# Delta-rule layer of a hybrid decoder: 16x16 block inverses on VectorE joined by TensorE, and products in a fixed alternating order

## The chip, the cores and the metric

The kernel runs on one core of a Trainium2 chip. The metric is the device time of one execution in microseconds (us). Engines are called TensorE (PE), VectorE (DVE), ScalarE (ACT), GpSimd (POOL) and SyncE (SP); PEld is TensorE's loading of weights.

## What is computed

A trunk of four layers over 1024 steps of 1024 channels in fp32: a short convolution, an S5 layer, the delta-rule layer (RWKV-7) and a convolution again. The delta-rule layer has 16 heads of 64 channels and carries a 64x64 state per head through the steps:

```python
def _rwkv_step(state, inp):
    r_t, w_t, k_t, v_t, kk_t, a_t = inp
    sa = einsum("bhvk,bhk->bhv", state, -kk_t)
    state = (state * w_t[:, :, None, :] + sa[..., None] * (kk_t * a_t)[:, :, None, :]
             + v_t[..., None] * k_t[:, :, None, :])
    out = einsum("bhvk,bhk->bhv", state, r_t)
    return state, out
...
r, k, v, z = einsum("nbld,nde->nble", xs[:4], w_rkvz)     # xs: mixes of x with its shift
kk = heads(k * k_k) / norm;   decay = exp(-exp(w_log))
out = scan(_rwkv_step, zeros, (r, decay, k, v, kk, a))
```

## The kernel before

*Chunks.* The 1024 steps are done in two halves h of 512, the heads in 8 pairs m, so there are 16 head pairs, in two loops of 8. A pair's 512 steps are 8 chunks of 64. Within a chunk the delta rule is a triangular system: with M the strictly lower 64x64 matrix of scores between kk·a and kk, the chunk's updates are T times a right side, where T is the inverse of identity minus M. So each pair needs 16 inverses (8 chunks, 2 heads); they lie side by side as blocks on the 128 partitions.

*The steps of a pair, with their lines.*
- `use_k`, `use_r`: the products with the weights of k and r, each split into high and low parts: 48 products of 128x512 per pair (L308 to L310), and decays, norms and scalings on VectorE and ScalarE.
- `prep`: two groups of score products (`s1`, L1673; 8 products each into two PSUM tiles, one per head); VectorE masks them into `sca` (L1677), ScalarE copies the other half out as `scr` (L1679), and copies the diagonal 32x32 blocks into `dg` (L1686) and the block below them into `m10` (L1688); VectorE transposes `dg` into `mi` (L1690). GpSimd masks `scr` (L1682) and scales `kb` by the decay (L1692). Then the transposes `kbtp` (L1697) and the value products `wps` (L1708).
- `tsolve`: VectorE inverts the 32x32 diagonal blocks, by three steps inside groups of four rows (L1728, L1731) and eight steps of product, reduction and addition over the groups (L1739 `tv`, L1744 `td`, L1745 `ti`). One partition holds one block's row, so all blocks advance together.
- `join`: two inverses of 32 become one of 64. VectorE transposes (L1754 `tt`, L1759 `t1`), TensorE forms the lower block by two rounds of 32x32 products (`zp` L1767, `tp` L1775), ScalarE copies between. Then the value and query products of the chunks (L1791, L1797) into `R.p1`, which L1785 clears, and `a2`.
- `seq`: the recurrence, 8 chunks one behind the other: a product with the state (L1818), a copy on ScalarE (L1819), a product that gives the update (L1822), the state's addition on VectorE (L1825). Output products (L1832), their copy (L1835) and transposes `otp` (L1860) follow.

*The order of work.* The steps are generators. `pull` issues one piece of another generator between two pieces of the current one, so the code order is an interleaving. A scheduler then orders the instructions of each engine by priority; `prio(generator, PJ)` raises a generator's instructions by an offset. `issue_after` adds an edge: what is issued in its body stands behind a given instruction. Each engine runs its list strictly in that order. In pair m the loop issues `use_k` and `use_r` (pulling the recurrence of pair m−2), then `prep(m)` pulling what is left of `tsolve(m−1)`, then `join(m−1)`, and puts `seq(m−1)` and `tsolve(m)` on the lists to be pulled from.

*PSUM.* Three tiles of 512 columns (`mm`) serve the large products, two (`aux`) all of prep's and join's products in turn, one (`sq`) outputs, two `R.p1`. A group that takes a tile waits until the reader of its former use is done.

Of the kernel before, what the change touches and what calls it, by code (L numbers as in the profile page):

```python
# [15 lines left out]
P = 128  # L16
# [282 lines left out]
def mm3(S, w, rhs, name, ms=0, half=None):  # L299
# [13 lines left out]
    return ps  # L313

# [920 lines left out]
PS, PT, PJ = 300, 300, 600  # L1235
# [53 lines left out]
def rwkv_layer(S, X, bg, l, last, nxt):  # L1289
# [9 lines left out]
    dST = dram_list(S, "dST", [P, P])  # L1299
    rgs = ExitStack()  # L1300
    rg = rgs.enter_context(S.tc.tile_pool(name="rg", bufs=1))
    C = S.rw
    C.ones = rg.tile([P, P], F32, tag="c_ones", name="c_ones")
    G.memset(C.ones, 0.0)
    G.memset(C.ones[0:64, 0:64], 1.0)
    G.memset(C.ones[64:P, 64:P], 1.0)
    C.ones_r = rg.tile([P, P], F32R, tag="c_ones_r", name="c_ones_r")
    G.tensor_copy(C.ones_r, C.ones)
# [173 lines left out]
    for h in range(2):  # L1482
# [130 lines left out]
def inner_setup(S, rg, T_):  # L1613
# [33 lines left out]

    zero = rg.tile([P, 2], F32, tag="zero", name="zero")
    G.memset(zero, 0.0)

    def prep(m, h, R):
# [4 lines left out]
        dg = rg.tile([P, 8, 32], F32, tag="dg", name="dg")  # L1656
        R.m10 = rg.tile([P, 8, 32], F32, tag="m10", name="m10", bufs=2)
        for w in range(2):
# [6 lines left out]
        for w in range(2):  # L1665
# [4 lines left out]
            for c in range(4):  # L1670
                for hd in range(2):
                    rows = slice(hd * 64, hd * 64 + 64)
                    nc.tensor.matmul(pss[hd][:, c * P:(c + 1) * P], kb[rows, 2 * c + w, :], ra[rows, 2 * c + w, :],  # L1673
                                     start=True, stop=True)
# [9 lines left out]
            for jb in range(2):  # L1684
                q = slice(w * 64 + jb * 32, w * 64 + jb * 32 + 32)
                SC.copy(dg[q], a[q, :, :, jb * 32:jb * 32 + 32].rearrange("p c d s -> p (c d) s"))  # L1686
            q = slice(w * 64, w * 64 + 32)
# [6 lines left out]
        for g in range(2):  # L1694
            ps = aux("kbtp")
            for i in range(4):
                nc.tensor.transpose(ps[:, i * P:(i + 1) * P], kb[:, 4 * g + i, :], S.ident)  # L1697
# [5 lines left out]
        pss = [aux("wps"), aux("wps")]  # L1703
        for c in range(4):
            for hd in range(2):
                for w in range(2):
                    rb, rk = rows_b[w], rows_k[w]
                    nc.tensor.matmul(pss[w][rb, c * P + hd * 64:c * P + hd * 64 + 64], sca[rk, w, c, hd, :],  # L1708
                                     R.uv[w][rk, c, hd * 64:hd * 64 + 64], start=True, stop=True)
        for w in range(2):  # L1710
            rb = rows_b[w]
            SC.copy(R.uv[w][rb].rearrange("p a b -> p (a b)"), pss[w][rb, :])
        yield

    def tsolve(R):

        mi = R.mi
        m0 = mi[:]

        rows4 = mi.rearrange("p (b r) s -> p b r s", r=4)  # L1720
        for q in range(3):
            n, ts = 3 - q, []
            for hf in range(2):
                c = 16 * hf + 16
                t = rg.tile([P, 4, 3, 32], F32, tag="tv", name="tp", bufs=2)[:, :, 0:n, 0:c]
                coef = bass.AP(m0.tensor, m0.offset + 528 * hf + 33 * q + 32, [list(m0.ap[0]), [132, 4], [32, n], [0, c]])
                rows = rows4[:, 4 * hf:4 * hf + 4, :, 0:c]
                V.tensor_tensor(t, rows[:, :, q, :].unsqueeze(2).to_broadcast([P, 4, n, c]), coef, ALU.mult)  # L1728
                ts.append((rows[:, :, q + 1:4, :], t))
            for r, t in ts:  # L1730
                V.tensor_tensor(r, r, t, ALU.add)  # L1731
            yield
        ti = R.ti = rg.tile([P, 8, 32], F32, tag="ti", name="ti")
        SC.copy(ti, eye)
        for b in range(7, -1, -1):
            n, c = 8 - b, 4 * b + 4
            t = rg.tile([P, 320], F32, tag="tv", name="tv", bufs=2)
            tv = t[:, 0:n * c * 4].rearrange("p (i c q) -> p i c q", i=n, q=4)
            V.tensor_tensor(tv, ti[:, b:8, 4 * b:4 * b + 4].unsqueeze(2).to_broadcast([P, n, c, 4]),  # L1739
                            mi[:, 4 * b:4 * b + 4, 0:c].rearrange("p q c -> p c q").unsqueeze(1).to_broadcast([P, n, c, 4]),  # L1740
                            ALU.mult)
            d = rg.tile([P, 96], F32, tag="td", name="td", bufs=2)
            dv = d[:, 0:n * c].rearrange("p (i c) -> p i c", i=n)
            V.tensor_reduce(dv, tv, mybir.AxisListType.X, ALU.add)  # L1744
            V.tensor_tensor(ti[:, b:8, 0:c], ti[:, b:8, 0:c], dv, ALU.add)  # L1745
            yield

    def join(m, h, R):
        ra, ti = R.ra, R.ti
        tt = slot(S, ("a0", "a1")[h], "tt")  # L1750
        tt = R.tt = tt.rearrange("p (h c) -> p h c", h=8)

        for jb in range(2):
            V.transpose(tt[:, :, jb * 32:jb * 32 + 32].rearrange("p h (i d) -> p i d h", d=4), ti)  # L1754
        yield

        t1 = rg.tile([P, 8, 32], F32, tag="tv", name="t1", bufs=2)
        zs = t1
        V.transpose(t1, tt[:, :, 0:32])  # L1759
# [5 lines left out]
        for e in range(8):  # L1765
            for w in range(2):
# [130 lines left out]
```

## Time and profile before

| | |
|---|---|
| three runs | 2867.61, 2871.57, 2873.37 us (median 2871.57) |
| the profiled execution | 2874.98 us, span 2873.3 us |
| TensorE busy | 2722.6 us (95%), weight loads 2163.6 us (75%) |
| VectorE, ScalarE, GpSimd busy | 1886.0 (66%), 1121.9 (39%), 635.8 us (22%) |
| mean granted TensorE clock | 0.88 in 1290 to 1560 us, 0.89 in 1780 to 2060 us (the two loops of head pairs) |

Shares of busy time are means over layers with different limits. The delta-rule loops are read by themselves, by stretches of the trace. A wait is put down to the instruction whose end came last before the waiting one began. A line at an engine is written as engine, tile, line, the tile it waits for; the numbers behind a wait are its sum in us, its count and the longest.

### The profile page before, as it was taken

Reading aid. Unit: us, or ns where it says so; the run is one execution under the profiler, and the core shown is the slowest. Engines: PE = TensorE matmul, PEld = TensorE weight load, DVE = VectorE, ACT = ScalarE, POOL = GpSimd, SP = SyncE. Lnnn points to the kernel's source line nnn. Section 1 sums busy time; section 2 is a strip of 40 time slices with the busy share of each in tenths; the row PEclk is TensorE's granted clock in tenths of the full one; section 3 lists DMA queues with packets and bytes.
Section 4 is the critical chain, followed back from the end, with each engine's and each line's share of the span. In section 5 each row is a group of like instructions: output and inputs, shape, how many; then the busy total and the mean of one; then the engine's idle time right before and its main releaser. Section 6 shows DMA issues by size and latency. Waiting matters only on the chain.

```text
span 2873.3 us, 40597 instructions
## 1 busy us (share of the span) xinstructions
PE 2722.6 (95%) x15131; PEld 2163.6 (75%) x15131; DVE 1886.0 (66%) x3428; ACT 1121.9 (39%) x2147; POOL 635.8 (22%) x690
## 2 busy tenths in 40 slices
PE   8999999999999999999888799898889999999998
PEld 6877788878877887577666577666667778888887
DVE  6787765477657347878788676887848473333654
ACT  3333322242144223655556465565534231112322
POOL 1243423221207033104333101333232210000000
PEclk9999999999999999999997799997899999999999
DMA  5333322358783333463222254222334332112320
GB/s 166 98 95 96 94 77 62 88 152 225 209 247 124 103 92 119 144 214 96 73 81 89 69 182 141 74 86 83 110 92 143 104 91 59 44 46 64 118 66 37
DMA packets 449749, 312.67 MB, mean 109 GB/s; under 512 B 48360, under 2 KB 393744, under 8 KB 449552
## 3 DMA queue, kind: packets, MB, share of 16 engines
q1 hardware_dynamic: 449552, 310.08, 36.0%
q8 instruction: 119, 1.95, 0.3%
q14 instruction: 78, 0.64, 0.1%
HBM read 240.28 MB, written 69.21 MB: 108 GB/s over the span
## 4 chain that ended last, share of the span: by engine, by line
PE 73%; DVE 14%; ACT 4%; issue 3%; POOL 2%; DMA 2%; SPq 0%; DVEq 0%; POOLq 0%; ACTq 0%
PE op L309 3%; PE op L308 3%; PE op L310 3%; PE gp L310 3%; PE zp L308 3%; PE gp L309 3%; PE zp L309 3%; PE zp L310 3%; PE gp L308 3%; PE sp L308 3%; PE sp L309 3%; PE sp L310 3%; DVE tv L1739 2%; PE hp L308 2%; PE hp L309 2%
## 5 line engine op out<-in xcount | busy, mean ns | idle before, releaser
L286 DVE TENSOR_TENSOR wl<-wraw,wh 128x1024 fp32r<-128x1024 f32 x283 | 365.9, 1294 | 311.5 <-ACT wh L285 303.5
L285 ACT CAST wh<-wraw 128x1024 fp32r<-128x1024 f32 x283 | 296.9, 1050 | 695.5 <-PE gp L309 191.8
L608 POOL TENSOR_TENSOR ln_s<-ln_s,rp 128x512 f32<-128x512 f32 x42 | 60.1, 1430 | 209.8 <-DVE rp L604 209.8
L1825 DVE SCALAR_TENSOR_TENSOR state<-state,pc,p 64x64 f32<-64x64 f32 x256 | 71.0, 277 | 50.1 <-PE p L1822 45.6
L1739 DVE TENSOR_TENSOR tv<-ti,mi 128x128 f32<-128x128 f32 (+3 forms) x128 | 97.1, 759 | 2.4
L1818 PE MATMUL p<-state,ra 128*128 128x128 f32 x256 | 65.7, 344 | 27.3 <-DVE state L1825 25.2
L1819 ACT COPY uv<-p 64x128 f32<-64x128 f32 x128 | 33.2, 259 | 138.8 <-PE p L1818 138.1
L1818 PEld LDWEIGHTS p<-state,ra 128*128 128x128 f32 x256 | 46.3, 219 | 52.7 <-DVE state L1825 42.1
L1673 PEld LDWEIGHTS s<-ra,kb 64*128 64x128 f32 x512 | 64.2, 212 | 20.4 <-ACT scr L1679 6.5
L1673 PE MATMUL s<-ra,kb 64*128 64x128 f32 x512 | 74.7, 314 | 4.4 <-ACT scr L1679 2.1
L1822 PE MATMUL p<-uv,kbt 128*128 128x128 f32 x256 | 67.7, 351 | 10.4 <-ACT uv L1819 10.3
L310 PE MATMUL gp<-r_0h,wl 128*128 128x512 f32 x192 | 76.9, 400 | 0.0
L308 PE MATMUL zp<-x_0h,wh 128*128 128x512 f32 x192 | 76.7, 400 | 0.0
L309 PE MATMUL gp<-r_0l,wh 128*128 128x512 f32 x192 | 76.7, 399 | 0.0
L308 PE MATMUL gp<-r_0h,wh 128*128 128x512 f32 x192 | 76.5, 398 | 0.0
L308 PE MATMUL gp<-r_1h,wh 128*128 128x512 f32 x192 | 76.4, 398 | 0.0
L310 PE MATMUL gp<-r_1h,wl 128*128 128x512 f32 x192 | 76.0, 396 | 0.1
L623 POOL TENSOR_TENSOR rp<-r_0h,r_0l 128x512 f32<-128x512 f32 x24 | 37.4, 1589 | 174.9 <-PE op L309 174.9
L308 PE MATMUL zp<-x_1h,wh 128*128 128x512 f32 x192 | 75.9, 396 | 0.0
L310 PE MATMUL zp<-x_1h,wl 128*128 128x512 f32 x192 | 75.8, 395 | 0.0
L309 PE MATMUL zp<-x_1l,wh 128*128 128x512 f32 x192 | 75.7, 394 | 0.0
L310 PE MATMUL zp<-x_0h,wl 128*128 128x512 f32 x192 | 75.7, 394 | 0.0
(740 smaller groups left out, 8437.6 us busy)
## 6 DMA issues: line engine op xcount, KB each, us to landing
wraw<-in_conv_w_in_dram SPq DMA_DIRECT2D x80, 512.0 KB
wraw<-in_rwkv_w_rkvz_dram SPq DMA_DIRECT2D x64, 512.0 KB
wraw<-in_ple_gate_dram SPq DMA_DIRECT2D x56, 512.0 KB
wraw<-in_conv_w_out_dram SPq DMA_DIRECT2D x24, 512.0 KB
wraw<-in_ssm_w_in_dram SPq DMA_DIRECT2D x21, 512.0 KB
xt<-xd SPq DMA_DIRECT2D x32, 256.0 KB
wraw<-in_rwkv_w_out_dram SPq DMA_DIRECT2D x16, 512.0 KB
wraw<-in_ple_proj_dram SPq DMA_DIRECT2D x14, 512.0 KB
```

Of the source, the lines that this page charges most:

```text
L285: nc.scalar.copy(wh, raw)
L286: nc.vector.tensor_tensor(wl, raw, f32(wh[:]), ALU.subtract)
L308: nc.tensor.matmul(ps, lh, xh, start=(k == 0), stop=False)
L309: nc.tensor.matmul(ps, lh, xl, start=False, stop=False)
L310: nc.tensor.matmul(ps, ll, xh, start=False, stop=(k == kt - 1))
L608: nc.gpsimd.tensor_tensor(s, s, rs, ALU.add)
L623: (eng or nc.gpsimd).tensor_tensor(rs, f32(rh[:]), f32(rl[:]), ALU.add)
L1673: nc.tensor.matmul(pss[hd][:, c * P:(c + 1) * P], kb[rows, 2 * c + w, :], ra[rows, 2 * c + w, :], start=True, stop=True)
L1739: V.tensor_tensor(tv, ti[:, b:8, 4 * b:4 * b + 4].unsqueeze(2).to_broadcast([P, n, c, 4]), mi[:, 4 * b:4 * b + 4, 0:c].rearrange("p q c -> ...
L1818: nc.tensor.matmul(p1, R.ra[:, c, :], st, start=False, stop=False, skip_group_check=True)
L1822: last = nc.tensor.matmul(p2[:, 0:P], R.kbt[c // 4][:, c % 4, :], uv, start=True, stop=True)
L1825: V.scalar_tensor_tensor(st[cs, cs], st[cs, cs], R.pc[cs, c:c + 1], p2[cs, cs], ALU.mult, ALU.add)
```

## The change

*The inverse.* `tsolve` now inverts the two 16x16 blocks on the diagonal of each 32x32 block, both in one instruction where it can: three steps inside groups of four rows and four steps (in place of eight) over the groups. ScalarE copies the 16x16 block below the diagonal into `R.nz`, in the place where it stands in the 32x32 block (`nzs`, cleared once ahead of the loops). `join` begins with a new stage on TensorE: 32 products of 32x32 (`low`) and four of 32x256 that add the identity (`eye32`) give `zi`, ScalarE copies it, 64 products of 32x32 (`full_t`, `full_u`) give the inverse of the 32x32 block and its transpose (`ut`), and ScalarE copies these out. One of the three VectorE transposes goes. From `zp` on all is as before.

*The order within groups.* `run_of` issues a list of products, each group behind the one before; with `order=True` each product stands behind the one before it by an edge. Scores and value products alternate between the two halves of the array (`hd` or `w` in the inner place). The row parts of `wps`, `zp` and `tp`, which had a PSUM tile each, now share one.

*The order of steps.* `join(m−1)` stands ahead of `prep(m)`, `prep` pulls the recurrence in place of `tsolve`, and the offset PJ is 4000.

```diff
+def run_of(S, steps, order=False):
+    behind, last = S.run, None
+    for step in steps:
+        after = last if order and last is not None else behind
+        if after is None:
+            last = step()
+        else:
+            with S.tc.issue_after(after.ins):
+                last = step()
+    S.run = last
...
-PS, PT, PJ = 300, 300, 600
+PS, PT, PJ = 300, 300, 4000
...
-                for _ in prio(I.prep(m, h, R), PJ):
-                    pull(tsol, TQ)
-                    pull(nxt_b)
                 while tsol:
                     pull(tsol)
                 if m > 0:
                     for _ in prio(I.join(m - 1, h, Rs[m - 1]), PJ):
                         pass
                     inner.append(prio(I.seq(m - 1, h, Rs[m - 1], ...), PS))
+                for _ in prio(I.prep(m, h, R), PJ):
+                    pull(nxt_b)
+                    pull(inner)
                 tsol.append(prio(I.tsolve(R), PT))
...
+    nzs = [rg.tile([P, 8, 32], F32, tag=f"nz{i}", name=f"nz{i}") for i in range(2)]
+    for t in nzs:
+        G.memset(t, 0.0)
...
-            for c in range(4):
-                for hd in range(2):
...
-                    nc.tensor.matmul(pss[hd][...], kb[rows, 2 * c + w, :], ra[rows, 2 * c + w, :], ...)
+            run_of(S, [lambda c=c, hd=hd: s1(c, hd) for c in range(4) for hd in (1, 0)], True)
...
                 SC.copy(dg[q], a[q, :, :, jb * 32:jb * 32 + 32]...)
+                q = slice(w * 64 + jb * 32, w * 64 + jb * 32 + 16)
+                SC.copy(R.nz[q, :, 16:32], a[q, :, :, jb * 32 + 16:jb * 32 + 32]...)
...
-        pss = [aux("wps"), aux("wps")]
...
+        ps = aux("wps")
+        run_of(S, [lambda ...: wv(c, hd, w) for c in range(4) for hd in range(2) for w in (1, 0)], True)
...
-        for b in range(7, -1, -1):
-            n, c = 8 - b, 4 * b + 4
+        for b in range(3, -1, -1):
+            n, c = 4 - b, 4 * b + 4
+            t = rg.tile([P, 192], F32, tag="tv", name="tv", bufs=2)
+            for k in range(2):
+                V.tensor_tensor(tv, x, y, ALU.mult)       # block k of the two
+            V.tensor_reduce(d, t..., ALU.add)             # both blocks
+            V.tensor_tensor(x, x, d..., ALU.add)
...
+        V.transpose(ub..., ti)
+        V.transpose(t1, ub)
+        ps = aux("zi")
+        low = lambda e, q: matmul(ps[q, cl(e)], R.nz[q, e, :], t1[q, e, :], ...)
+        eye32 = lambda q: matmul(ps[q, 0:256], S.ident[q, q], S.ident[q, q]..., ...)
+        run_of(S, [low(e, q) for e in range(8) for q in quad] + [eye32(q) for q in quad])
+        SC.copy(zi..., ps[:, 0:256])
+        ps2 = aux("ut")
+        full_t = lambda e, q: matmul(ps2[q, cl(e + 8)], ub[q, e, :], zi[q, e, :], ...)
+        full_u = lambda e, q: matmul(ps2[q, cl(e)], zi[q, e, :], ub[q, e, :], ...)
+        run_of(S, [f(e, q) for f in (full_t, full_u) for e in range(8) for q in quad])
+        SC.copy(t1..., ps2[:, 256:512])
+            SC.copy(tt[:, :, jb * 32:jb * 32 + 32], ps2[:, 0:256]...)
-        ps = [aux("zp"), aux("zp")]
+        ps3 = aux("zp")
...
-        ps = [aux("tp"), aux("tp")]
+        ps4 = aux("tp")
```

*What moves, on three places.* In all three the place is the second half, about the fifth pair. A row is the line, the operation, the tile written and the tiles read, the shape and the count of such instructions in a row. First TensorE's list before, where the scores of a pair (L1673, tiles s) are issued, amid the recurrence of an earlier pair (L1818, L1822) and large products (L308 to L310):

```order
L1673 MATMUL s_17485<-ra,kb 128x128 x4
L1818 MATMUL p_17154<-state,ra 128x128
L309 MATMUL sp<-xs1l,wh 128x512
L310 MATMUL sp<-xs1h,wl 128x512
L1822 MATMUL p_17290<-uv,kbt 128x128
L308 MATMUL sp<-xs1h,wh 128x512
L1673 MATMUL s_17508<-ra,kb 128x128 x4
L1818 MATMUL p_17153<-state,ra 128x128
L309 MATMUL sp<-xs1l,wh 128x512
L310 MATMUL sp<-xs1h,wl 128x512
L1673 MATMUL s_17509<-ra,kb 128x128 x4
L1822 MATMUL p_17296<-uv,kbt 128x128
```

And the same place after (scores L1691, recurrence L1857 and L1861, transposes kbtp L1718):

```order
L1861 MATMUL p_18166<-uv,kbt 128x128
L1691 MATMUL s_18180<-ra,kb 128x128
L1857 MATMUL p_18099<-state,ra 128x128
L1691 MATMUL s_18179<-ra,kb 128x128
L1691 MATMUL s_18180<-ra,kb 128x128
L1691 MATMUL s_18179<-ra,kb 128x128
L1691 MATMUL s_18180<-ra,kb 128x128
L1691 MATMUL s_18179<-ra,kb 128x128
L1691 MATMUL s_18180<-ra,kb 128x128
L1691 MATMUL s_18179<-ra,kb 128x128
L1861 MATMUL p_18191<-uv,kbt 128x128
L1718 MATMUL kbtp<-ident,kb 128x128 x4
```

The large products that stood between the score groups and ahead of kbtp are gone from there, and the scores alternate between their two tiles one by one.

Second, TensorE's list in the join before:

```order
L308 MATMUL sp<-xs0h,wh 128x512
L1767 MATMUL zp<-t_17565,m_17022 32x32 x7
L1785 MATMUL p_17610<-zero,ident 128x2
L1767 MATMUL zp<-t_17565,m_17022 32x32 x9
L309 MATMUL sp<-xs0l,wh 128x512
L310 MATMUL sp<-xs0h,wl 128x512
L308 MATMUL sp<-xs0h,wh 128x512
L1775 MATMUL tp<-tt,t_17565 32x32 x16
```

And the join after, with the new stage (zi L1783 and L1785, ut L1792 and L1793), output transposes otp (L1899) and zp (L1808):

```order
L308 MATMUL sp<-xs1h,wh 128x512
L309 MATMUL sp<-xs1l,wh 128x512
L310 MATMUL sp<-xs1h,wl 128x512
L1783 MATMUL zi<-t_18497,nz_9912 32x32 x32
L1785 MATMUL zi<-ident 32x256 x4
L308 MATMUL sp<-xs1h,wh 128x512
L309 MATMUL sp<-xs1l,wh 128x512
L310 MATMUL sp<-xs1h,wl 128x512
L1792 MATMUL ut<-zi,ub 32x32 x32
L1793 MATMUL ut<-ub,zi 32x32 x32
L1899 MATMUL otp<-ident,o 128x128 x4
L1808 MATMUL zp<-t_18603,m_18141 32x32 x16
```

Three large products stand ahead of zi and three between zi and ut; behind ut follow otp and zp.

Third, ScalarE's list ahead of the second score group after (scr L1698, dg L1705, nz L1707, m10 shown as m L1709, uv L1858):

```order
L1698 COPY scr<-s_18148 128x4x64
L1705 COPY dg<-sca 32x256
L1707 COPY nz_9912<-sca 16x8x16
L1705 COPY dg<-sca 32x256
L1707 COPY nz_9912<-sca 16x8x16
L1709 COPY m_18141<-sca 32x256
L1698 COPY scr<-s_18147 128x4x64
L1858 COPY uv<-p_18099 64x128
```

The copy that frees the group's second PSUM tile (the second scr row) stands behind five copies out of sca, two of them new.

More of the change, by code (lines that the diff above doesn't have):

```diff
@@ L1299, in rwkv_layer @@
     dST = dram_list(S, "dST", [P, P])
+    S.run = None
     rgs = ExitStack()
@@ L1718, in tsolve @@
         m0 = mi[:]
-        rows4 = mi.rearrange("p (b r) s -> p b r s", r=4)
+        part = list(m0.ap[0])
         for q in range(3):
[L1722 to L1731, printed above, removed]
+            n = 3 - q
+            r = []
+            for k in range(2):
+                rows = lambda i, st: bass.AP(m0.tensor, m0.offset + 528 * k + 32 * i, [part, [128, 4], [st, n], [1, 16]])
+                ck = bass.AP(m0.tensor, m0.offset + 528 * k + 33 * q + 32, [part, [132, 4], [32, n], [0, 16]])
+                t = rg.tile([P, 4, 3, 16], F32, tag="tv", name="tp", bufs=2)[:, :, 0:n, :]
+                V.tensor_tensor(t, rows(q, 0), ck, ALU.mult)
+                r.append((rows(q + 1, 32), t))
+            for x, y in r:
+                V.tensor_tensor(x, x, y, ALU.add)
             yield
@@ L1751, in join @@
         tt = R.tt = tt.rearrange("p (h c) -> p h c", h=8)
+        ub = rg.tile([P, 8, 32], F32, tag="ub", name="ub")
+        V.transpose(ub.rearrange("p h (i d) -> p i d h", d=4), ti)
+        t1 = rg.tile([P, 8, 32], F32, tag="tv", name="t1", bufs=2)
+        V.transpose(t1, ub)
+        quad = [slice(32 * q, 32 * q + 32) for q in range(4)]
+        ps = aux("zi")
+        cl = lambda e: slice(e * 32, e * 32 + 32)
+        low = lambda e, q: nc.tensor.matmul(ps[q, cl(e)], R.nz[q, e, :], t1[q, e, :], start=(e == 0), stop=False,
+                                            skip_group_check=True)
@@ new lines, in join @@
+        eye32 = lambda q: nc.tensor.matmul(ps[q, 0:256], S.ident[q, q], S.ident[q, q].unsqueeze(1).to_broadcast([32, 8, 32]),
+                                           start=False, stop=True, skip_group_check=True)
+        run_of(S, [lambda e=e, q=q: low(e, q) for e in range(8) for q in quad] + [lambda q=q: eye32(q) for q in quad])
+        zi = rg.tile([P, 8, 32], F32, tag="ti", name="zi")
+        SC.copy(zi.rearrange("p h c -> p (h c)"), ps[:, 0:256])
+        yield
+        ps2 = aux("ut")
```

103 lines of the change are left out of this document (52 added, 51 removed).

## The prediction

> **What bounds the kernel now.** I read the page's first part, then busy time and granted clock by stretch, then what TensorE waits for inside the delta-rule loops, then the order of single instructions in one steady head pair.
>
> ```profile
> span 2873.3 us, 40597 instructions
> PE 2722.6 (95%) x15131; PEld 2163.6 (75%) x15131; DVE 1886.0 (66%) x3428; ACT 1121.9 (39%) x2147; POOL 635.8 (22%) x690
> ```
> ```profile
> core 0: us, PE busy (x) PEld busy (x) DVE busy (x) ACT busy (x) POOL busy (x), PEclk, DMA share, GB/s
> 1290.00:1560.00 270.00, 236.24 (x2113) 186.64 (x2112) 219.78 (x495) 149.59 (x383) 92.76 (x96) 0.88 0.29 87
> 1780.00:2060.00 280.00, 248.20 (x2346) 190.95 (x2345) 235.03 (x535) 155.16 (x416) 95.08 (x93) 0.89 0.27 85
> 1899.00:1935.70 36.70, 33.29 (x340) 24.57 (x340) 32.25 (x78) 22.02 (x63) 13.60 (x14) 1.00 0.28 89
> 1469.90:1473.30 3.40, 3.40 (x68) 2.75 (x68) 2.11 (x6) 2.35 (x12) 0.94 (x4) 1.00 0.02 5
> 1473.30:1476.70 3.40, 3.40 (x62) 2.69 (x63) 3.37 (x15) 0.90 (x4) 1.04 (x1) 0.50 0.00 0
> ```
> The change touches only the two loops, 1290 to 1560 and 1780 to 2060 us, seven to eight head pairs each. There TensorE is busy 236 of 270 us and VectorE 220; in one undisturbed pair (the third row, full clock) it is 33.3 and 32.3 of 36.7. So TensorE bounds, with VectorE close behind. The mean clock of 0.88 to 0.89 is a third loss. The last two rows show one way into it: 3.4 us of unbroken work, nearly all of it products of 32x32 blocks (rows below), after which the granted clock is 0.50. The two loops are 550 us for 15 of the 16 pairs, so each us per pair is 16 us, 0.56% of the time.
>
> ```profile
> PE p L1818 <- DVE state L1825: 9.0, 9, 2.2
> PE kbtp L1697 <- POOL kb L1692: 4.7, 3, 2.8
> PE zp L1767 <- DVE t L1759: 2.3, 3, 1.8
> PE sp L308 <- DVE aq L1411: 2.2, 1, 2.2
> ...
> PE kbtp L1697 <- POOL kb L1692: 7.5, 8, 1.4
> PE p L1818 <- DVE state L1825: 3.9, 5, 1.1
> PE s L1673 <- DVE kb L1429: 1.9, 3, 0.7
> PE zp L1767 <- DVE t L1759: 1.6, 1, 1.6
> PE pb L1449 <- DVE kk L1426: 1.5, 2, 0.9
> ```
> These are TensorE's waits in the two loops (first four rows the first loop). On VectorE's results it waits 9.0+2.3+2.2+3.9+1.9+1.6+1.5 = 22.4 us, on GpSimd's scaled kb 12.2.
>
> **The change, part by part.** *VectorE's saving.* Groups of VectorE:
> ```profile
> L1739 DVE TENSOR_TENSOR tv<-ti,mi 128x128 f32<-128x128 f32 (+3 forms) x128 | 97.1, 759 | 2.4
> L1744 DVE TENSOR_REDUCE td<-tv 128x32 f32<-128x128 f32 (+3 forms) x128 | 51.0, 398 | 2.1
> L1745 DVE TENSOR_TENSOR ti<-ti,td 128x32 f32<-128x32 f32 (+3 forms) x128 | 47.1, 368 | 2.6
> L1744 DVE TENSOR_REDUCE td<-tv 128x32 f32<-128x128 f32 x32 | 9.1, 283 | 0.5
> L1728 DVE TENSOR_TENSOR tp<-mi 128x64 f32<-128x64 f32 x16 | 3.5, 216 | 0.0
> L1754 DVE STREAM_TRANSPOSE tt<-ti 128x256 f32<-128x256 f32 x32 | 17.2, 612 | 1.4 <-PE p L1822 1.2
> ```
> The first three are 195.2 us, 12.2 per pair. After it there are 8 products of 64 to 96 elements (216 ns by the fifth row, about 240 for the wider), 4 reductions of 128 to 192 (283 to about 350), 4 additions (about 220): 1.8+1.3+0.9 = 4.0. Halving the widest rows of the first three steps saves some 0.8, one transpose fewer 0.6. In all 9.6 us per pair of some 31 (235 us over 7.6 pairs). That is no time by itself, TensorE being the bound. It shortens waits: of the 22.4 us at most all come back (24 for 16 pairs), at least none. I take three quarters, **-17**, since a wait behind a queue of half the length rarely stays whole.
>
> *TensorE's new work.* 96 products of 32x32 per pair, two instructions each, so 192, and four of 32x256.
> ```profile
> 1500.38 0.69 PE L1767 MATMUL zp<-t,m 32*32 32x32 f32 x32
> 1501.01 0.50 PE L310 MATMUL sp<-xs0h,wl 128*128 128x512 f32 x1
> ...
> 1470.84 0.69 PE L1767 MATMUL zp<-t,m 32*32 32x32 f32 x16
> 1471.45 0.49 PE L310 MATMUL sp<-xs1h,wl 128*128 128x512 f32 x1
> ...
> 1913.85 1.16 PE L1673 MATMUL s<-ra,kb 64*128 64x128 f32 x8
> 1914.93 0.49 PE L1818 MATMUL p<-state,ra 128*128 128x128 f32 x2
> ...
> 1918.18 0.40 PE L308 MATMUL sp<-xs1h,wh 128*128 128x512 f32 x1
> 1919.26 1.09 PE L1697 MATMUL kbtp<-ident,kb 128*128 128x128 f32 x8 [0.68 <-POOL kb L1692]
> ```
> From start to next start, 32 such instructions took 0.63 us (20 ns each) where two parts of the array were used in turn, 16 took 0.61 (38 ns) where one part was used over and over. The new ones go round four quarters. I take 20 ns, 3.8 us; ends 10 ns (1.9 us, if four parts give double again) and 38 ns (7.3). The wide ones: a 512-column product spans about 0.23 us; eight instructions of at most that, four side by side, 0.5, at most 1.8.
>
> *Alternation.* The scores now stand four of one half in a row: eight instructions in 1.08 us (1913.85 to 1914.93), four such groups per pair. By the ratio 20 to 38, alternating saves about half, 2.0 us per pair; at least nothing. The value products (L1708) already alternate in part; 0.3. TensorE's net is 3.8+0.5-2.0-0.3 = +2.0 per pair, **+32** in all (low end near 0, high end 9.1 per pair, a rival below). Nothing covers it where TensorE is the bound.
>
> A rule speaks against more than that. The Trainium skill, TensorEngine Tiling (Array Packing), section Restrictions and Gotchas, says that different row tiles cannot access the same PSUM bank at the same time. The changed joins and value products send all row parts to one PSUM tile, where before they had one each. By that rule the joins would cost what one part alone costs, 7.3 us; no row of this run has two row parts in one bank, so the trace cannot decide it.
>
> *The moved order.* Before, large products (L308 to L310) stand between the score groups and ahead of kbtp. After, prep follows join at once: scores, kbtp and value products have hardly any between them.
> ```profile
> L1686 ACT COPY dg<-sca 32x256 f32<-32x256 f32 x64 | 25.7, 401 | 4.4 <-DVE sca L1677 3.7
> L1679 ACT COPY scr<-s 128x256 f32<-128x256 f32 x64 | 23.1, 369 | 32.8 <-DVE sca L1677 28.6 <-PE p L1832 3.8
> L1688 ACT COPY m<-sca 32x256 f32<-32x256 f32 x32 | 12.9, 403 | 0.6
> L1819 ACT COPY uv<-p 64x128 f32<-64x128 f32 x128 | 33.2, 259 | 138.8 <-PE p L1818 138.1
> L1682 POOL TENSOR_TENSOR scr<-scr,mask 128x512 f32<-128x512 f32 x32 | 46.1, 1442 | 56.5 <-ACT scr L1679 56.1
> L1692 POOL TENSOR_TENSOR kb<-kb,pc 128x1024 f32<-128x1024 f32 x16 | 31.3, 1957 | 9.2 <-PE s L1673 9.1
> ```
> The second score group needs the two buffers of the first. ScalarE frees the second of them only behind dg, nz, dg, nz, m: from the group's end about 0.65 (drain, mask), 0.37, 0.80, 0.52 (nz like uv's 259 ns), 0.40, 0.37 = 3.1 us. Then 0.9 of scores. GpSimd masks scr (1.44 from 3.1) and then scales kb (1.96), so kbtp starts 6.5 us after the first group. TensorE has some 2.0 us of its own in that time: 4.5 idle, against 0.8 per pair on kb now (12.2 over 15). Queued behind kbtp are the next state product and all large products. The first pair of each half keeps large products there and the last two or three pairs have few left anywhere, where the recurrence sets the pace; eight pairs stay. Ends 0 and 3.7 each; I take the middle, 1.8: **+14**. The new steps of the join (transposes, zi, ut, copies) have three large products or otp as cover. In four pairs without large products that cover is gone, and two more drains and copies of about 0.4 add some 2 us: **+8**. ScalarE's other new copies (some 3 us per pair, at 155 of 280 us busy) cost nothing further.
>
> *Clock.* The join's new stretch of small blocks, about 7 us with three large products in it, is longer than the stretch that halved the clock at 1473.3. A 3.4 us stretch at half clock loses at most 1.7. Ends 0 and 27 (once per pair); I take one more in every fourth pair, **+7**.
>
> *A stall.* In the sixth pair one step of the recurrence took 18.7 us:
> ```profile
> 1553.24 0.49 PE L1818 MATMUL p<-state,ra 128*128 128x128 f32 x2
> ...
> 1571.95 0.49 PE L1818 MATMUL p<-state,ra 128*128 128x128 f32 x2 [0.82 <-DVE state L1825]
> ```
> In the changed order the mixes for the next half stand apart on VectorE with state updates between them: **-15** (a step of 3.7 left); ends 0 and -16.
>
> No DMA is added; SP's loads move with their pairs and stay ahead of use. GpSimd's two memsets lie ahead of the loop. The sum: -17+32+14+8+7-15 = +29 against the profiled 2874.98 us, which stands 3.4 above the median, so 2871.6+29, about **2900 us**.
>
> **Rivals.** *Faster: VectorE was the bound in effect.* Net TensorE work of 0.6 per pair (+10), all waits on VectorE gone (-24), the stall gone (-15), no loss at kbtp: 2843 us. For it: VectorE at 88% in the undisturbed pair. Against it: that pair's TensorE is at 91%. It decides if the net is under 1 us per pair and kbtp starts within 3 us of the second score group's start.
> *Row parts wait for each other in one bank*: 3.5 more per pair for the joins and 0.5 for the value products, +60: about 2960. For it the skill's rule; against it, nothing measured.
> *The clock falls in every pair*, twice: 2 x 1.7 x 16 = 54 in place of 7, partly under idle time: about 2935. For it: the 0.50 above. The Trainium skill, TensorE: Matmul & The Clock Gate, section What's actually happening, has the clock set by recent activity in windows of about 3.4 us; the trace's stretch agrees in length, but it followed unbroken busy time, so small blocks seem to count for little.
> *The terms cancel* (no difference): about 2872, if the moved order costs nothing and a third of the new work hides under waits that stay.
>
> **How the numbers follow.** Forecast 0.42, faster rival 0.28, bank 0.08, clock 0.15, cancel 0.07. Slower by over 0.2% (5.7 us, about what a measurement here can tell from no change) is 0.42+0.08+0.15 = 0.65. The range goes from the faster rival's 2843, less 5 for its own spread, to 2945, which leaves out the bank case and edges. The forecast's own range is 2882 to 2925.
>
> **What would show it.** VectorE's sum for tv, td and ti near 64 us instead of 195; zi and ut 192 small instructions in about 4 us per pair (7 if the bank rule holds); eight score instructions in under 0.7 us; kbtp waiting on kb or scr for over 20 us in all instead of 12 to 14; mean clock in the loops at or below 0.88; no step over 10 us. The forecast is wrong if the pairs with 48 large products take 36 us or less.

## The result, and the profile after

The changed kernel takes 2897.82 us (median of 4 runs, 2895.33 to 2898.29) against 2869.59 before: a ratio of 1.0096, 95% interval 1.0078 to 1.0113. That is 28.2 us slower, where 2900 and +29 were forecast. The sum came out; the runs below show which of its terms did, and that terms of this kind do not add here.

The page's head and the stretches of the two loops, after (columns as before):

```profile
span 2893.6 us, 46955 instructions
PE 2740.5 (95%) x18331; PEld 2169.0 (75%) x18331; DVE 1784.3 (62%) x3284; ACT 1157.1 (40%) x2275; POOL 625.7 (22%) x692
```
```profile
1290.00:1560.00 270.00, 231.79 (x3239) 176.45 (x3238) 162.85 (x397) 150.78 (x411) 84.83 (x92) 0.87 0.29 89
1780.00:2060.00 280.00, 238.76 (x3506) 182.93 (x3506) 171.75 (x441) 158.14 (x445) 84.86 (x90) 0.87 0.24 73
1387.50:1390.90 3.40, 2.29 (x20) 1.65 (x19) 0.93 (x4) 3.33 (x10) 1.72 (x2) 1.00 0.38 128
1390.90:1394.30 3.40, 1.94 (x8) 1.67 (x8) 2.89 (x5) 3.33 (x9) 1.54 (x2) 0.50 0.00 0
1394.30:1397.70 3.40, 3.40 (x39) 2.79 (x38) 3.40 (x5) 2.41 (x7) 2.94 (x3) 0.50 0.00 0
```

VectorE is busy 335 of 550 us in the loops instead of 455. TensorE issues 3200 instructions more. The last three rows are one place that comes back in most pairs: scores with waits between them, then half clock for 6.8 us. In ten of the 16 pairs all eight instructions of kbtp start under half clock. The timeline of TensorE there (start, duration, line, tile, count, idle before and what ended it):

```profile
1389.16 1.16 PE L1691 MATMUL s<-ra,kb 64*128 64x128 f32 x14 [0.94 <-ACT scr L1698]
1390.24 0.49 PE L1861 MATMUL p<-uv,kbt 128*128 128x128 f32 x2
1392.36 1.11 PE L1718 MATMUL kbtp<-ident,kb 128*128 128x128 f32 x4 [1.63 <-POOL kb L1713]
...
1394.56 1.05 PE L1718 MATMUL kbtp<-ident,kb 128*128 128x128 f32 x4
1395.54 1.97 PE L1727 MATMUL wps<-uv,sca 64*64 64x64 f32 x32
```

So kbtp and the value products run at half clock. TensorE's groups, before and then after (busy, mean ns, idle before them and what ended it):

```profile
L1673 PE MATMUL s<-ra,kb 64*128 64x128 f32 x512 | 74.7, 314 | 4.4 <-ACT scr L1679 2.1 <-DVE kb L1429 1.9 <-DVE kp L1453 0.4
L1697 PE MATMUL kbtp<-ident,kb 128*128 128x128 f32 x128 | 22.8, 317 | 17.9 <-POOL kb L1692 12.1 <-ACT scr L1679 4.2 <-POOL pt L1397 1.6
L1767 PE MATMUL zp<-t,m 32*32 32x32 f32 x512 | 15.5, 204 | 4.1 <-DVE t L1759 4.0
L1775 PE MATMUL tp<-tt,t 32*32 32x32 f32 x512 | 16.2, 205 | 0.1
L1818 PE MATMUL p<-state,ra 128*128 128x128 f32 x256 | 65.7, 344 | 27.3 <-DVE state L1825 25.2 <-ACT ra L1800 2.0
```
```profile
L1691 PE MATMUL s<-ra,kb 64*128 64x128 f32 x512 | 59.8, 320 | 15.8 <-ACT scr L1698 11.8 <-ACT ra L1839 4.0
L1718 PE MATMUL kbtp<-ident,kb 128*128 128x128 f32 x128 | 30.8, 388 | 23.6 <-POOL kb L1713 17.1 <-POOL pc L1416 2.7 <-ACT scr L1698 2.1
L1793 PE MATMUL ut<-ub,zi 32*32 32x32 f32 x1024 | 14.8, 202 | 5.5 <-issue 5.4
L1792 PE MATMUL ut<-zi,ub 32*32 32x32 f32 x1024 | 13.4, 202 | 3.0 <-ACT zi L1789 3.0
L1814 PE MATMUL tp<-tt,t 32*32 32x32 f32 x512 | 13.0, 204 | 5.1 <-ACT t L1811 3.6 <-issue 1.3
L1808 PE MATMUL zp<-t,m 32*32 32x32 f32 x512 | 13.0, 204 | 1.1 <-issue 1.1
L1783 PE MATMUL zi<-t,nz 32*32 32x32 f32 x1024 | 12.5, 197 | 1.4 <-DVE t L1778 1.1
L1785 PE MATMUL zi<-ident 32*32 32x256 f32 x128 | 11.0, 402 | 0.0
L1857 PE MATMUL p<-state,ra 128*128 128x128 f32 x256 | 64.7, 339 | 7.6 <-DVE state L1864 7.2
```

The recurrence waits 20 us less for the state, the scores 11 and kbtp 6 more. "issue" is idle time in which nothing in the profile is waited for.

To weigh the parts, TensorE's time from the layer's first large product (sp) to its last gate product (gp) is split three ways, from every instruction's start to the next start: idle time, time under half clock, time under full clock. Half of the half-clock time is counted as lost to the clock, which is an upper value for small products. "Work" is the rest. Differences to before (1517.6 work, 82.1 clock, 106.9 idle: 1706.6 us), with the time of the whole kernel as its ratio. One profiled execution stands behind each split, so differences of a few us between rows are not to be read:

| kernel | ratio (95%) | work | clock | idle |
|---|---|---|---|---|
| changed: inverse, alternation, order | 1.0096 (1.0078 to 1.0113) | +15.7 | +4.6 | +3.7 |
| alternation alone | 1.0049 (1.0037 to 1.0061) | -23.0 | +10.8 | +21.9 |
| order of steps alone | 1.0125 (1.0105 to 1.0146) | -20.6 | +11.5 | +38.0 |
| inverse alone | 1.0180 (1.0167 to 1.0193) | +57.2 | +5.2 | -13.1 |
| inverse, alternation | 1.0167 (1.0151 to 1.0183) | +20.1 | +12.7 | +10.2 |
| alternation, order | 1.0255 (1.0234 to 1.0275) | -41.5 | +70.6 | +43.2 |
| changed, VectorE's work back | 1.0556 (1.0534 to 1.0577) | +1.8 | +77.3 | +85.3 |
| changed, ut twice | 1.0433 (1.0412 to 1.0454) | +24.9 | +65.3 | +35.9 |
| changed, early copies | 1.0119 (1.0099 to 1.0138) | +13.1 | +5.7 | +9.8 |
| alternation, no edges between groups | 1.0043 (1.0031 to 1.0056) | -16.3 | +2.3 | +21.9 |
| changed, half of ut | 1.0087 (1.0073 to 1.0102) | +8.0 | +8.4 | +7.9 |
| changed, no edges between groups | 1.0128 (1.0112 to 1.0143) | +18.9 | +14.0 | +4.1 |
| changed, spare large products | 1.0115 (1.0098 to 1.0132) | +49.6 | -8.6 | -4.3 |

### The profile page after: what moved, and what is told of

It is laid out like the page before. It is cut to its first block, busy times and chain, and to the rows that moved or that the text cites. A ratio compares the mean times of both kernels' runs of the same rounds, so it can differ in the third digit from the quotient of the medians.

```text
span 2893.6 us, 46955 instructions
## 1 busy us (share of the span) xinstructions
PE 2740.5 (95%) x18331; PEld 2169.0 (75%) x18331; DVE 1784.3 (62%) x3284; ACT 1157.1 (40%) x2275; POOL 625.7 (22%) x692
## 5 line engine op out<-in xcount | busy, mean ns | idle before, releaser
L1696 DVE TENSOR_TENSOR sca<-s,mask 128x256 f32<-128x256 f32 x64 | 24.6, 420 | 131.5 <-PE s L1691 131.5
L1864 DVE SCALAR_TENSOR_TENSOR state<-state,pc,p 64x64 f32<-64x64 f32 x256 | 71.1, 278 | 28.0 <-PE p L1861 23.6
L308 PE MATMUL zp<-x_0h,wh 128*128 128x512 f32 x192 | 76.7, 400 | 0.0
L1701 POOL TENSOR_TENSOR scr<-scr,mask 128x512 f32<-128x512 f32 x32 | 41.3, 1289 | 163.9 <-ACT scr L1698 163.9
L310 PE MATMUL gp<-r_0h,wl 128*128 128x512 f32 x192 | 76.4, 398 | 0.0
L308 PE MATMUL gp<-r_1h,wh 128*128 128x512 f32 x192 | 76.4, 398 | 0.0
L310 PE MATMUL gp<-r_1h,wl 128*128 128x512 f32 x192 | 76.1, 396 | 0.1
L308 PE MATMUL zp<-x_1h,wh 128*128 128x512 f32 x192 | 76.0, 396 | 0.0
L310 PE MATMUL zp<-x_1h,wl 128*128 128x512 f32 x192 | 75.9, 395 | 0.0
L308 PE MATMUL gp<-r_0h,wh 128*128 128x512 f32 x192 | 75.8, 395 | 0.0
L310 PE MATMUL zp<-x_0h,wl 128*128 128x512 f32 x192 | 75.8, 395 | 0.0
L309 PE MATMUL zp<-x_0l,wh 128*128 128x512 f32 x192 | 75.6, 394 | 0.0
L309 PE MATMUL gp<-r_1l,wh 128*128 128x512 f32 x192 | 75.4, 393 | 0.0
L1691 PE MATMUL s<-ra,kb 64*128 64x128 f32 x512 | 59.8, 320 | 15.8 <-ACT scr L1698 11.8
L1861 PE MATMUL p<-uv,kbt 128*128 128x128 f32 x256 | 67.6, 350 | 6.6 <-ACT uv L1858 6.5
L1858 ACT COPY uv<-p 64x128 f32<-64x128 f32 x128 | 33.3, 260 | 99.4 <-PE p L1857 98.3
```

Source lines behind the costliest of these rows:

```text
L308: nc.tensor.matmul(ps, lh, xh, start=(k == 0), stop=False)
L309: nc.tensor.matmul(ps, lh, xl, start=False, stop=False)
L310: nc.tensor.matmul(ps, ll, xh, start=False, stop=(k == kt - 1))
L1691: return nc.tensor.matmul(pss[hd][:, c * P:(c + 1) * P], kb[rows, 2 * c + w, :], ra[rows, 2 * c + w, :], start=True, stop=True)
L1701: G.tensor_tensor(r8, r8, mask[:, 1, :].unsqueeze(1).to_broadcast([P, 8, CH]), ALU.mult)
L1858: SC.copy(uv[rb, :], p1[rb, :])
```

## The experiments

**Alternation alone.** The kernel before with `run_of` and the shared tiles, without the 16x16 inverse and the new order of steps.

```diff
-            for c in range(4):
-                for hd in range(2):
+            run_of(S, [lambda c=c, hd=hd: s1(c, hd) for c in range(4) for hd in (1, 0)], True)
```

> The kernel before with the alternating order of products alone (scores, value products, joins, shared PSUM tiles); inversion of 32x32 and order of steps as before. Theory (TensorE's own time sets the pace of the loops): the scores fall from 71 to about 56 us in sum as they did in the changed kernel, the value products by 1 to 3, so about 17 us less than before, 2849 to 2857. Rival (VectorE or the recurrence sets the pace, and TensorE waits longer instead): within 5 us of before's 2869.6.

2884.92 us, slower than before. From start to next start, idle time left out, the scores fell from 71.3 to 60.6 us (56 was expected) and the value products from 27.2 to 22.1, and the time did not fall: work is 23 us less, but idle 22 more and the clock 11 worse. TensorE was not the bound in the sense that its own time sets the pace. Its waits grew by 4 to 6 us each in several places: ahead of the scores (4.4 to 9.9), of otp (14.2 to 18.4) and of these two, which had waited 2.4 and 2.6:

```profile
L1463 PE MATMUL pb<-kph,c_ones_r 128*128 128x512 f32 x16 | 7.6, 472 | 7.7 <-DVE kk L1440 6.9 <-DVE td L1757 0.8
L308 PE MATMUL sp<-xs0h,wh 128*128 128x512 f32 x128 | 56.8, 444 | 6.5 <-DVE aq L1425 6.1 <-ACT xs0h L191 0.4
```

**The order of steps alone.** The kernel before with join ahead of prep, prep pulling the recurrence, and the offset 4000. The three were not separated.

```diff
+                for _ in prio(I.join(m - 1, h, Rs[m - 1]), PJ): ...
                 for _ in prio(I.prep(m, h, R), PJ):
```

> The kernel before with the new order of steps alone (join ahead of prep, prep pulls the recurrence, offset 4000). Theory: waits at the second score group and at kbtp rise by about 17 us, waits of the recurrence fall by about 24, and since VectorE still takes 12 us per pair for the inversion, which is now drained ahead of the join, TensorE waits for it at the join: 10 to 30 us slower than before, 2880 to 2900. Rival 1 (the waits only change places): within 5 us of before. Rival 2 (the order is the gain of the change, the small products its loss): 15 us or more faster, under 2855.

2906.85 us, a little above the theory's range. The waits at the join came: zp waited 16.8 us instead of 4.1, the clearing product of p1 13.4 instead of 1.0, and the update product 24.0 instead of 10.4. The state product waited 11.1 instead of 27.3. But the 17 us of new waits at the scores and kbtp did not come with the order alone: together they waited 14.8 us, less than the 22.3 before.

**The inverse alone.**

```diff
-    (run_of with order, shared tiles, join ahead of prep, offset 4000)
+    (their form before); tsolve, nz, zi and ut as changed
```

> The changed kernel with the order of steps, the order of single products and the PSUM tiles of before: only the 16x16 inversion and TensorE's new stage are left of the change. Theory: the new small products cost 43 us of TensorE, of which waits on VectorE (22 us before) give back up to 17: 2890 to 2913. Rival (VectorE was the bound in effect): 2870 or less.

2922.45 us, +51, above the theory's range. Idle falls by 13, towards the 17 of the term for VectorE; work rises by 57. The new products are 43 of that; zp (13.9 to 20.8 us), wps (27.2 to 32.3) and tp also take longer in this list.

**Inverse and alternation, order of before.**

```diff
-PS, PT, PJ = 300, 300, 4000          (and join ahead of prep)
+PS, PT, PJ = 300, 300, 600           (and prep ahead of join)
```

> The changed kernel with the order of steps of before (prep ahead of join, offset 600); inversion and alternation as changed. Theory (the forecast's term for the moved order, +14 and +8 less 15 for the stall): 5 to 25 us faster than the changed kernel's 2897.8, so 2873 to 2893. Rival (the new order of steps pays by itself, by keeping the recurrence fed): as slow as the changed kernel or slower, 2898 or more.

2918.44 us: the rival holds. With the short inversion the new order is a gain of 20 us, not the loss that was forecast.

**Alternation and order, 32x32 inversion.**

```diff
-    tsolve and join over 16x16 blocks
+    tsolve and join over 32x32 blocks, as before
```

> The kernel before with alternation, shared PSUM tiles and the new order of steps, but the 32x32 inversion on VectorE. With this every combination of the three parts but one has a time. Theory (in the new order the inversion lies on the path, since it is drained ahead of the join): TensorE waits for VectorE at the joins as in the run of the order alone (zp 16.8 us of waits there), so 2905 to 2930, and the 16x16 inversion saves 8 to 30 us in this order in spite of its 43 us of new products. Rival (the 16x16 inversion is a loss in any order): 2893 or less.

2944.89 us: beyond the theory's range, in its direction. The 16x16 inverse alone costs 51 us in the old order and saves 47 in the new one with alternation. Most of the 47 is the clock (66 less) and idle time (40 less) against 57 more work.

**VectorE's work given back.**

```diff
+                for _ in range(3):
                     V.tensor_tensor(t, rows(q, 0), ck, ALU.mult)
...
+                for _ in range(2):
                     V.tensor_tensor(tv, x, y, ALU.mult)     # and the reduction td twice
```

> The changed kernel with VectorE's saving given back: in the inversion each product of the first three steps is made three times, each product and reduction of the later ones twice, some 10 us more of VectorE per pair. Theory (VectorE's inversion ends ahead of its use only just in the new order): 15 to 40 us slower than the changed kernel, 2913 to 2938. Rival (the saving is off the path, TensorE being the bound): within 5 us of 2897.8.

3031.27 us, 133 more than the changed kernel and far above the theory. By the groups of VectorE the five lines of the inversion take 250.7 us instead of 152.7, 6.1 us per pair and not the 10 expected; each pair pays 8.3. TensorE's waits in that run:

```profile
L1786 PE MATMUL zi<-t,nz 32*32 32x32 f32 x1024 | 14.3, 212 | 19.2 <-DVE t L1781 19.1
L1817 PE MATMUL tp<-tt,t 32*32 32x32 f32 x512 | 15.5, 220 | 15.0 <-ACT t L1814 12.5 <-issue 2.4
L1902 PE MATMUL otp<-ident,o 128*128 128x128 f32 x64 | 12.5, 326 | 36.0 <-POOL o L1895 36.0
```

The first products of the join now wait 19 us for the inversion (1.4 before the edit). The longest wait is that of the output transposes for GpSimd's o, 36.0 us against 4.9; GpSimd in turn waits 31.4 us for VectorE's gn_s instead of 15.3. It seems that VectorE's longer inversion also holds up its other work. The clock falls with the idle time: 365 us at half clock between 1290 and 2150 us, 201 in the changed kernel.

**The ut products twice.**

```diff
-for f in (full_t, full_u) for e in range(8) for q in quad])
+for f in (full_t, full_u, full_t, full_u) for e in range(8) for q in quad])
```

> The changed kernel with the 64 products ut of each pair made twice, which doubles 24 us of TensorE's new work. Theory (TensorE's products in the join are on the path and paid in full): 18 to 28 us slower, 2916 to 2926. Rival (other waits shrink in their place, as the 12 us that alternation saved came back as 22 us of waits): within 8 us of 2897.8.

2996.94 us: 99 more, four times what was added. Work rose by 9, the loss to the clock by 61, idle time by 32. Ahead of ut itself TensorE stood idle 47.5 us instead of 8.5:

```profile
L1793 PE MATMUL ut<-ub,zi 32*32 32x32 f32 x2048 | 31.0, 208 | 27.1 <-issue 27.1
L1792 PE MATMUL ut<-zi,ub 32*32 32x32 f32 x2048 | 28.8, 205 | 20.4 <-issue 17.2 <-ACT zi L1789 3.3
```

All but 3.3 us of this waits for no engine and no transfer of data. The stretch outruns the supply of its instructions, and the traces bear that out. The page counts 160 instruction transfers of 16 KB on queue 8 (144 in the changed kernel, 119 before), which is one for every 256 further instructions of TensorE, weight loads included (6400 more in the changed kernel, 4096 more here). Between 1290 and 2200 us this run has 24 stops of over 0.4 us with nothing else waited for, 44.4 us in all; the changed kernel has 8 (7.3 us), the kernel before none. Every one of these 32 ends 1.2 to 1.6 us after such a transfer has landed; of this run's 73 other waits as long, one does. No run changed the supply itself.

**Copies that free the score tiles first.** ScalarE's dg, nz and m behind all four scr copies, GpSimd's kb ahead of its second mask.

```diff
+    scaled = G.tensor_tensor(kb, kb, R.pc..., ALU.mult)          # ahead of the second scr mask
+    with S.tc.issue_after(freed[0].ins), S.tc.issue_after(freed[1].ins):
         SC.copy(dg[q], ...); SC.copy(R.nz[q, ...], ...); SC.copy(R.m10[q], ...)
```

> The changed kernel with ScalarE's copies of dg, nz and m put behind all four copies that free the score tiles, and GpSimd's scaling of kb ahead of its second masking. Theory (the waits of the second score group on scr, 15.8 us, and of kbtp on kb and scr, 23.6 us, are on the path): most of the first and a third to two thirds of the second go, 15 to 30 us faster, 2868 to 2883. Rival (TensorE then waits for something else just behind, the value products or the recurrence): within 6 us of 2897.8.

2905.74 us: not faster, within 8 us of the changed kernel, a little beyond the rival's bound. The waits did go, and came back one step on:

```profile
L1692 PE MATMUL s<-ra,kb 64*128 64x128 f32 x512 | 48.2, 298 | 1.7 <-ACT ra L1842 1.1 <-ACT scr L1699 0.6
L1721 PE MATMUL kbtp<-ident,kb 128*128 128x128 f32 x128 | 19.2, 298 | 10.2 <-POOL kb L1701 10.2
L1422 PE MATMUL pss<-c_ones_r,sq 128*128 128x2 f32 x128 | 21.9, 293 | 14.2 <-ACT sq L1419 14.2
L1860 PE MATMUL p<-state,ra 128*128 128x128 f32 x256 | 69.0, 358 | 29.4 <-DVE state L1867 29.1 <-ACT ra L1842 0.3
```

Scores and kbtp wait 11.9 us instead of 39.4; the state product waits 29.4 instead of 7.6 and pss 14.2 instead of 1.2.

**Alternation without edges between groups.** Against the run of alternation alone:

```diff
-        after = last if order and last is not None else behind
+        after = last if order else None          # groups are not tied to each other
```

> As the run of alternation alone (2884.9 us), but each group's order holds only inside the group: no edge ties a group of products behind the group before it, and value, query and join products are free again. Theory (the edges between groups cost the 22 us of waits that came with alternation alone, TensorE's saving of 12 us being real): 2850 to 2866, faster than before. Rival (shorter scores only lay open waits that stood behind them, and lower the granted clock): 2878 to 2892, as with the edges.

2884.41 us, the rival: the edges are not what alternation's waits come from; idle time is again 22 us above before. Why shorter scores lay open that much waiting stays open.

**Half of the ut products.**

```diff
-for f in (full_t, full_u) for e in range(8) for q in quad])
+for f in (full_u,) for e in range(8) for q in quad])
+        V.transpose(t1, tt[:, :, 0:32])
```

> The changed kernel with half of the ut products: TensorE makes only the block inverses (32 products of 32x32 per pair in place of 64), and VectorE transposes them, 0.6 us per pair. Theory (small products cost a multiple of their own time, through the empty instruction supply behind them and the granted clock, as 24 us more of them cost 99): 12 us less of them makes it 20 to 50 us faster, 2848 to 2878. Rival 1 (paid at their own size, 10 to 13 us): 2885 to 2888. Rival 2 (VectorE's transpose is waited for, since it stands between ut and zp): 2895 or more.

2896.07 us, not told apart from 2897.82: less work (8 us), as much more clock loss and idle time. Doubling cost 99 us and halving saved nothing, so no one price per product fits both. The two edits are not mirror images, though. The stops for want of instructions are gone here, and the transpose that VectorE does instead stands waiting for ScalarE's copy:

```profile
L1798 DVE STREAM_TRANSPOSE t<-tt 128x256 f32<-128x256 f32 x16 | 7.1, 444 | 16.6 <-ACT tt L1797 16.6
```

What half of the products alone would save therefore stays open. Rival 2's number fits, its reason does not: zp waited 0.0 us in that run.

**The changed kernel without edges between groups.**

```diff
-    run_of(S, [... s1 ...], True)  (and wv, values, queries, S.run in kbtp)
+    run_free(S, [... s1 ...], True)          # order inside the group only
```

> The changed kernel without the edges that tie scores, kbtp, value and query products behind the group before; the order inside the scores and the value products stays. Theory (where prep follows join at once the groups stand in this order anyway): within 6 us of 2897.8. Rival (the edges cost here what they may cost in the order of before): 10 us or more faster, under 2888.

2908.95 us: neither. The edges, which were thought neutral, are worth 11 us here, most of it clock (9 us).

**Spare large products in the stretch from scores to kbtp.**

```diff
+            if w == 1:
+                spare(pss[1])                # four products of 128x512 ahead of the scores
...
+            if g == 0:
+                spare(ps)                    # four ahead of kbtp
```

> The changed kernel with eight more products of 128x512 per pair whose results are overwritten: four ahead of the second score group, in the tile that its first products then write, and four ahead of kbtp, in kbtp's first tile. They put work of the full array into the stretch from the scores to kbtp, from which the new order took the large products, at 0.23 us each, 1.9 us per pair, 30 us in all. Theory (that stretch lowers the granted clock for 6.8 us in nearly every pair, which costs up to 3.4 us): half-clock time in the two loops falls from 201 us to under 130, and most of the new work stands in waits for scr and kb; 5 to 40 us faster, 2858 to 2893. Rival (the clock falls for another reason, or stays down): half-clock time stays near 200 us and the new work is paid, 15 to 35 us slower, 2913 to 2933.

2907.71 us: neither range. Half-clock time between 1290 and 2150 us fell from 201 to 160 us. In the loops the clock rose to 0.93 and 0.90:

```profile
1290.00:1560.00 270.00, 234.28 (x3279) 176.44 (x3280) 156.07 (x396) 147.49 (x403) 82.77 (x90) 0.93 0.27 83
1780.00:2060.00 280.00, 246.55 (x3342) 186.78 (x3341) 162.89 (x420) 152.57 (x419) 83.82 (x87) 0.90 0.25 76
```

Of kbtp's 128 instructions 34 start under half clock instead of 91, of the value products' 512 only 40 instead of 360. So filling this stretch with large products keeps the clock up on kbtp and wps. Taking its waits away does so too: with the early copies 15 of kbtp's and 96 of the value products' start under half clock, but there the fall comes one step on, at the transposes prn and antp (58 and 56 of 64, 15 and 12 in the changed kernel). The spare products add 34 us of work, not 30, and clock and idle time give back 21: filling costs more than it saves. No version here beats the kernel before.

## Why the prediction was right, and where it was right by its sum only

By the split above, work rose by 15.7 us, the loss to the clock by 4.6 and idle time by 3.7. The forecast had +32, +7 and, with its other four terms together, -10. The direction and the price of the new products were reasoned; that the sum came within 2 us is luck, since the errors cancel.

**VectorE's saving (-17).** Its size per pair was a little off: the lines of the inversion and their transposes went from 281 us (257.8 and 23.6, by VectorE's groups) to 170, 7.0 us per pair and not 9.6. The step that failed is the claim that the first three steps get shorter; they got longer, 62.6 to 79.4 us:

```profile
L1728 DVE TENSOR_TENSOR tp<-mi 128x192 f32<-128x192 f32 (+2 forms) x96 | 31.5, 351 | 18.3 <-PE tp L1775 16.6 <-ACT gsq L1846 1.1
L1731 DVE TENSOR_TENSOR mi<-mi,tp 128x192 f32<-128x192 f32 (+3 forms) x96 | 31.1, 351 | 0.7
```
```profile
L1748 DVE TENSOR_TENSOR tp<-mi 128x192 f32<-128x192 f32 (+2 forms) x96 | 44.6, 497 | 0.6
L1764 DVE TENSOR_TENSOR tv<-ti,mi 128x64 f32<-128x64 f32 (+1 forms) x128 | 37.8, 329 | 0.6
L1751 DVE TENSOR_TENSOR mi<-mi,tp 128x128 f32<-128x128 f32 (+2 forms) x96 | 34.8, 396 | 0.2
L1766 DVE TENSOR_REDUCE td<-tv 128x32 f32<-128x128 f32 (+1 forms) x64 | 20.3, 317 | 1.3
L1768 DVE TENSOR_TENSOR ti<-ti,td 128x32 f32<-128x32 f32 (+1 forms) x64 | 15.2, 238 | 1.3
```

These groups mix shapes. One shape is behind the rise, the products and additions of 192 elements (first row before, the others after):

```profile
L1728 DVE TENSOR_TENSOR tp<-mi 128x192 f32<-128x192 f32 x16 | 5.5, 341 | 0.3
```
```profile
L1748 DVE TENSOR_TENSOR tp<-mi 128x192 f32<-128x192 f32 x32 | 30.4, 990 | 0.1
L1751 DVE TENSOR_TENSOR mi<-mi,tp 128x192 f32<-128x192 f32 x32 | 21.2, 688 | 0.2
```
```profile
1869.86 2.70 DVE L1748 TENSOR_TENSOR tp<-mi 128x192 f32<-128x192 f32 x2
1869.74 1.26 POOL L1432 TENSOR_TENSOR ga<-ga,cs 128x512 f32<-128x512 f32 x1
1870.96 1.38 POOL L1445 TENSOR_TENSOR kb<-kp,cs 128x512 f32<-128x512 f32 x1
```

Of these 64 instructions after, 26 have no work of GpSimd beside them and take 348 to 361 ns. The 35 that take 526 to 1465 ns all have GpSimd at work beside them for at least 84% of their time, with products of two tiles (TENSOR_TENSOR) as in the last three rows; three others overlap with it in part and take 346 to 358 ns. Before, this shape stood nearly always beside nothing or beside GpSimd's clearings (MEMSET), and took 305 to 360 ns. The excess over 350 ns is some 31 us. Without it, by the durations of the undisturbed ones, the three steps would be 0.8 us per pair shorter, as the prediction has it. What it left out is that in the new order these steps stand beside GpSimd's products. Before, it was the later steps (tv and ti) that were stretched in this way, 55 instructions by some 42 us; after, 11 by 7. That GpSimd is the cause is read from the traces; no run moved its work away.

As waits, inverse alone gave 13 us. What was missed is its worth in the new order, where the inversion is drained ahead of the join: -47 net with alternation, and 133 for giving 6.1 us per pair back.

**TensorE's new work (+32).** Right as a net, +27, from terms mis-sized both ways. The new products cost 43 us (start to start, idle left out), not 69: 64 instructions of zi took 0.56 us undisturbed and 128 of ut 1.10, 9 ns each, the low end that was named (a product is two instructions). The scores saved 15.7 us, not 32: at full clock and without a wait one starts every 78 ns on average instead of every 111, which is not half. The value products saved 0.8, since 360 of 512 now start under half clock (65 before). The rule of the Trainium skill's TensorEngine Tiling (Array Packing), Restrictions and Gotchas, that different row tiles cannot access one PSUM bank at the same time, does not show as a cost: zp and tp, with both row parts in one tile, take 21 and 22 ns per instruction at full clock against 26 and 25 before.

**The moved order (+14) and the bare join (+8).** The first waits came about as priced: scores and kbtp wait 17.1 us more. They do not come from the order alone, with which these two waited less than before. The second came larger: ut, zi, tp and the value products of the join, which (as far as they were there) had waited 0.1 in all, wait 21. The step that failed is that such waits are time lost: taking 27 of them away gained nothing, and with the short inversion the new order gains 20 us.

**The clock (+7).** +4.6 by the split. The rival of a clock that falls in each pair is nearer to the picture, once per pair instead of twice; its price of 54 us was not. Between 1290 and 2150 us half-clock time rose from 188 to 201 us only, since the kernel before had already lost the clock 16 times there (19 times after). The Trainium skill's TensorE: Matmul & The Clock Gate, What's actually happening, has the clock fall after an idle window of some 3.4 us. Here a window with 2.29 of 3.40 us busy was enough, when the work was products of 64 rows.

**The stall (-15).** The step is gone: inside a pair no step of the recurrence exceeds 8.5 us (18.7 before). That it was worth 15 us does not show. From the first state product of the pair that had the stall to that of the second pair behind it, 84.3 us passed before and 88.3 us pass after. And the step from the last chunk of one pair to the first of the next grew: within a half it takes 16.8 us on average (13.8 to 20.3), before 11.2 (5.2 to 21.6).

**The signs named.** kbtp's waits in the loops are 23.4 us, the clock is 0.87, and the six pairs with 48 large products take 40.3 to 42.0 us (first state product to the next pair's first), none of them 36 or less. Eight score instructions take 0.63 us at full clock, under the 0.7 named. The sum of tv, td and ti is 73.3 us instead of the 64 named, and the small instructions of zi and ut take 2.1 us per pair, not 4.

The faster rival fell with the runs: each of the three parts alone is slower than before.

## What to carry to other kernels

Where an idle stretch lowers the clock and one pair's end feeds the next, the terms of a sum are not independent: parts that cost 51, 13 and 35 us alone cost 28 together. A forecast needs the combinations priced, above all which step is drained ahead of which. A wait that is measured is not yet time that can be won: follow what would be late next before counting it.

## What was not expected of the hardware

Instructions of 32x32 products going round four quarters of the array start every 9 ns, against 20 ns for two parts. A long run of them stops with nothing else waited for, 0.6 to 1.3 us at a time in the changed kernel and up to 5.0 us with 128 products in a row; each stop of over 0.4 us ended 1.2 to 1.6 us after 16 KB of instructions had landed. A product of 192 elements per partition on VectorE took about 350 ns with GpSimd idle or clearing a tile, and up to 1.4 us beside GpSimd's products of two tiles.
